# A decoder layer on one core: the first three column tiles of the gated MLP as plain products, the transformed activations made under them

## The chip, the cores and the metric

The kernel runs on one core of a Trainium2 chip. The metric is the device time of one execution in microseconds (us). The core has a matrix engine (TensorE, PE in the profile), an elementwise engine (VectorE, DVE), an engine for table functions and casts (ScalarE, ACT), a general one (GpSimd, POOL) and SyncE (SP), which here only issues transfers. Matmul results go to accumulators in PSUM, of which this kernel keeps two sets of four banks ("pa" and "pb"), each of 128 x 512 numbers.

## The reference

One decoder layer on x of 512 tokens by 2048 features. Cut to what matters:

```python
h = rmsnorm(x, g_mix) @ w_in            # four mixers on column groups: S5, Conformer, RG-LRU, pooling
x = x + concat(mixers(h)) @ w_out       # output projection and residual
h = rmsnorm(x, g_ffn)
gate, val = split(h @ w_up)             # 2048 -> 2 x 5504
gate = causal_dwconv(gate, w3, b3)      # width 3 along the tokens
x = x + (gelu(gate) * val) @ w_down     # 5504 -> 2048
out = rmsnorm(x, g_fin)
```

What follows concerns the seam between the output projection and `h @ w_up`, and the whole of `h @ w_up`.

## The kernel before

Activations are kept transposed: a row tile is 128 features by 512 tokens, sixteen of them for 2048 features. Precision is made up from a reduced 32-bit format: every operand is split into a high part (a cast, on ACT) and a low part (a subtraction, on DVE), and `mm3` (L98) issues three matmuls: high by high, high by low, low by high. Weights come in chunks of 128 x 1024 (512 KB): a load into a raw tile, the cast ("hi"), the subtraction ("lo").

**Output projection.** `quad(q, ...)` makes four of the sixteen output tiles at once in four pa banks. The last group of input rows is done in `tail` (L1037): for each q, 48 matmuls of 512 columns, then four residual additions into the tiles x2 (names A16 to A31 in the profile, pool `ar`), which free the banks, then `forms` for two pairs of row tiles and `square2`, which stores x2 to memory for the end of the layer and adds its squares to "rstd". The squares and the forms share one buffer, "hh".

**The MLP's first product.** `ffn_up` works through 43 column tiles f. Each has 128 gate and 128 value columns, and the inner dimension of 2048 is cut into two halves (even and odd row tiles; a pair p has one of each), so a tile has four weight blocks of 128 x 1024: a and b (gate, first and second half), c and d (value). Gate and value for both token halves are made in a Strassen-like way: seven products of 256 columns instead of eight. The weight forms are a, b, d as loaded, and r1 = c + d, r2 = r1 + a, r3 = c + a, r4 = r2 + b. For r1 and r3 the second block is added by an accumulating load from the GpSimd queue ("ur<-w_up"); r2 and r4 are sums on DVE. On the other side, `forms` makes for each pair p a tile X{p} of seven forms of the activations, each high and low, 256 tokens wide. A product is 24 matmuls (8 pairs by 3). The sequence per tile is a of f, d of f-1, r1 of f, r4 of f-1, r2, b, r3 of f. Sums of products are carried by accumulating in one bank and by copies on ACT: of the a bank after a (us), after a+r2 (uu) and after a+r2+r3 (uw); r1's bank is added to uw on DVE. After d and r4 the tile is finished: scaling by the norm's statistic, the convolution and the GELU, and the product with the value half, on DVE and ACT ("ug", "uc"). Each of these small tiles has two buffers. The last DVE product of a tile reads uw. The first half of the result is read straight from the a bank.

The norm's statistic need not be there before that: the weights act on x times g_ffn, and 1/rms is applied to the result. `rstd_bc` makes it: matmuls of ones with the summed squares, scaling, a square root on ACT, a reciprocal and three small steps on DVE ("tiny"), matmuls that broadcast it, a copy.

**What sets the order.** In `tail` a scheduler orders the instructions of each engine; loads and weight pieces are marked with a higher priority. Each engine then works its list in order. Raw weight tiles of `ffn_up` come from the pool `rp` with nine buffers, in the space that `ar` and `aq` leave; so the loads wait until the tiles there have been read. The d blocks use the two raw buffers of the chunk plan (`wp`); high and low parts have three buffers each (`wq`). `down`, the last product, has its weights in the chunk plan and reads the stored results back ("av", split to "Sh", "Sl"). Its first sweep accumulates in all eight banks.

## Time and profile before

| | us |
|---|---|
| median of 3 runs | 1954.33 (1952.54 to 1954.68) |
| profiled execution | 1953.47 |
| its span | 1951.7 |
| PE busy | 1869.0 (96%) |
| DVE busy | 1353.0 (69%) |
| ACT busy | 808.3 (41%) |

The span runs from the first to the last instruction; 1.8 us lie around it. The engines work beside each other, so their busy times overlap, and only what ends last in a stage sets its time. The output projection ends near 541 us, `ffn_up` runs to about 1462 us, and `down` follows it.

### The profile page before, as it was taken

Reading aid. Unit: us, or ns where it says so; the run is one execution under the profiler, and the core shown is the slowest. Engines: PE = TensorE matmul, PEld = TensorE weight load, DVE = VectorE, ACT = ScalarE, POOL = GpSimd, SP = SyncE. Lnnn points to the kernel's source line nnn. Section 1 sums busy time; section 2 is a strip of 40 time slices with the busy share of each in tenths; the row PEclk is TensorE's granted clock in tenths of the full one; section 3 lists DMA queues with packets and bytes.
Section 4 is the critical chain, followed back from the end, with each engine's and each line's share of the span. In section 5 each row is a group of like instructions: output and inputs, shape, how many; then the busy total and the mean of one; then the engine's idle time right before and its main releaser. Section 6 shows DMA issues by size and latency. Waiting matters only on the chain.

```text
span 1951.7 us, 29884 instructions
## 1 busy us (share of the span) xinstructions
PE 1869.0 (96%) x11878; PEld 1690.6 (87%) x11878; DVE 1353.0 (69%) x1997; ACT 808.3 (41%) x1064; POOL 171.3 (9%) x249
## 2 busy tenths in 40 slices
PE   7999999999928999999999999999999999999996
PEld 6788887888728999999999999999998888888886
DVE  8699989998766777777777777777765433333334
ACT  6323447432544444444444444444444222222232
POOL 6210020221001000000000000000000000000000
PEclk9999999999959999999999999999999999999998
DMA  5332323433428777776767777776738443333334
GB/s 200 99 94 89 103 90 112 142 90 94 146 78 226 190 204 188 196 204 186 209 184 206 189 195 205 190 211 182 200 100 275 135 146 108 113 108 98 98 97 141
DMA packets 106701, 298.62 MB, mean 153 GB/s; under 512 B 15233, under 2 KB 21377, under 8 KB 106561
## 3 DMA queue, kind: packets, MB, share of 16 engines
q1 hardware_dynamic: 92784, 249.78, 38.1%
q0 software_dynamic: 13488, 46.41, 14.4%
q8 instruction: 93, 1.52, 0.3%
q10 hardware_dynamic: 288, 0.52, 0.1%
q14 instruction: 48, 0.39, 0.1%
HBM read 274.51 MB, written 19.66 MB: 151 GB/s over the span
## 4 chain that ended last, share of the span: by engine, by line
PE 90%; DVE 6%; ACT 2%; DMA 1%; issue 1%; POOL 0%; DVEq 0%; POOLq 0%; ACTq 0%
PE pa L96 59%; PE pb L96 31%; DVE X L59 1%; DMA ur<-w_up 1%; DVE lo L59 1%; DVE o L59 0%; DVE rstd L59 0%; DVE bk L59 0%; DVE A L62 0%; ACT hi L105 0%; DVE l_x L62 0%; DVE M L59 0%; ACT hh L1076 0%; ACT A L72 0%; DVE A L59 0%
## 5 line engine op out<-in xcount | busy, mean ns | idle before, releaser
L96 PE MATMUL pa<-A,hi 128*128 128x512 f32 x1312 | 412.8, 397 | 11.5 <-ACT A L72 6.4
L59 DVE TENSOR_TENSOR lo<-raw,hi 128x1024 fp32r<-128x1024 f32 (+1 forms) x175 | 215.6, 1233 | 243.5 <-ACT hi L105 243.3
L105 ACT CAST hi<-raw 128x1024 fp32r<-128x1024 f32 (+1 forms) x175 | 183.0, 1046 | 458.7 <-PE pa L96 390.9
L59 DVE TENSOR_TENSOR ulr<-ur,uhr 128x1024 fp32r<-128x1024 f32 x172 | 210.4, 1223 | 149.0 <-ACT uhr L105 149.0
L96 PEld LDWEIGHTS pa<-A,hi 128*128 128x128 f32 x1312 | 247.0, 190 | 69.5 <-ACT A L72 7.3
L105 ACT CAST uhr<-ur 128x1024 fp32r<-128x1024 f32 x172 | 180.1, 1047 | 304.4 <-PE pa L96 150.4
L96 PE MATMUL pa<-X,uhr 128*128 128x256 f32 x1408 | 260.3, 285 | 6.6 <-ACT uhr L105 6.6
L96 PE MATMUL pa<-A,lo 128*128 128x512 f32 x656 | 257.5, 397 | 3.9 <-DVE lo L59 3.9
L96 PE MATMUL pb<-X,uhr 128*128 128x256 f32 x1344 | 246.4, 283 | 0.0
L96 PEld LDWEIGHTS pa<-X,uhr 128*128 128x128 f32 x1408 | 221.4, 193 | 6.8 <-ACT uhr L105 6.7
L96 PEld LDWEIGHTS pb<-X,uhr 128*128 128x128 f32 x1344 | 209.7, 192 | 0.0
L96 PE MATMUL pa<-X,ulr 128*128 128x256 f32 x704 | 200.1, 284 | 0.0
L96 PE MATMUL pb<-X,ulr 128*128 128x256 f32 x672 | 190.3, 283 | 0.0
L96 PEld LDWEIGHTS pa<-A,lo 128*128 128x128 f32 x656 | 124.4, 190 | 33.1 <-DVE lo L59 4.8
L1130 POOL DMA_DIRECT2D ur<-w_up x86 | 75.2, 874 | 857.5 <-DMA ur<-w_up 437.1
L96 PE MATMUL pa<-Sh,hi 128*128 128x512 f32 (+1 forms) x392 | 149.4, 382 | 0.0
L96 PE MATMUL pa<-Sl,hi 128*128 128x512 f32 (+1 forms) x392 | 149.2, 381 | 0.0
L96 PE MATMUL pa<-Sh,lo 128*128 128x512 f32 (+1 forms) x392 | 149.1, 381 | 0.0
L96 PEld LDWEIGHTS pa<-X,ulr 128*128 128x128 f32 x704 | 136.2, 193 | 0.0
L96 PEld LDWEIGHTS pb<-X,ulr 128*128 128x128 f32 x672 | 129.1, 192 | 0.0
L96 PE MATMUL pa<-X,uhb 128*128 128x256 f32 x688 | 126.1, 284 | 0.1
L96 PE MATMUL pb<-Sl,hi 128*128 128x512 f32 (+1 forms) x328 | 124.4, 379 | 0.0
(290 smaller groups left out, 3483.7 us busy)
## 6 DMA issues: line engine op xcount, KB each, us to landing
ur<-w_up SPq DMA_DIRECT2D x86, 512.0 KB, 5.9
ur<-w_up POOLq DMA_DIRECT2D x86, 512.0 KB, 7.3
raw<-w_dn SPq DMA_DIRECT2D x54, 512.0 KB, 3.8
ud<-w_up SPq DMA_DIRECT2D x43, 512.0 KB, 6.2
ua<-w_up SPq DMA_DIRECT2D x43, 512.0 KB, 4.7
ub<-w_up SPq DMA_DIRECT2D x43, 512.0 KB, 3.8
raw<-w_b SPq DMA_DIRECT2D x40, 512.0 KB, 3.7
raw<-w_out SPq DMA_DIRECT2D x32, 512.0 KB, 3.6
```

What stands on the lines that cost most here:

```text
L59: (eng or self.nc.vector).tensor_tensor(out, x, y, op=op)
L96: self.nc.tensor.matmul(ps, lhsT=l, rhs=r, start=start, stop=stop, skip_group_check=go_on)
L105: self.nc.scalar.copy(hi, src)
L1130: nc.gpsimd.dma_start(v8(t), blk(f, "d" if form == "r1" else "a"), accum_op=ADD)
```

## The change

Three things are changed.

1. The first three column tiles (NSTD = 3) are done in plain form by the new `ffn_std`: four weight blocks, each with all 512 tokens, eight pairs, three matmuls of 512 columns, so 96 matmuls a tile in two banks instead of 168 of 256 columns. Their weights are part of the chunk plan, behind w_out. The operand is taken from rows 0 and 6 (even row tiles) or 1 and 2 (odd row tiles) of X{p}. In the first tile, a and c take pairs 0 to 5 before 6 and 7, and `rstd_bc` stands between b and d.
2. `forms` becomes three steps. `forms1` makes the four plain forms straight from x2. `forms2` scales x2 in place and makes three of the transformed forms. `forms3` overwrites row 6, which the plain tiles read, with the last one, in the third tile. The squares get buffers of their own.
3. The residual tiles lie in pairs in the raw weight pool `rp` (now eight buffers of 128 x 1024), so a raw buffer comes free when `forms3` has read it; they are stored as eight pieces of 512 KB instead of sixteen of 256 KB. The small tiles of `ffn_up` are taken from the slots A8 to A15: us and uu become two halves of one tile (A12 and A13 in turn), uw is A14 alone, ug A8 and A9, uc A10 and A11, the statistic A15. PE's instructions of the whole tail keep the order in which the program issues them.

```diff
-MERGE = False
+NSTD = 3
...
+            self.blk = lambda f, x: a["w_up"][(NF if x in "cd" else 0) + f][:, 8 * (x in "bd"):8 * (x in "bd") + 8]
+            srcs += [self.blk(f, x) for f in range(NSTD) for x in "acbd"]
             self.plan(srcs)
...
-            self.tail()
+            with tc.manual_schedule(engines={mybir.EngineType.PE}):
+                self.tail()
...
-        self.x2 = []
+        self.x2, self.xp2 = [], []
+        self.ar.release()
+        self.rp = tc.alloc_tile_pool(name="rp", bufs=8, side="right", reuse_waits="tile")
...
-                        self.x2.append(self.at(16 + d, F32))
+                        if d % 2 == 0:
+                            self.xp2.append(self.rp.tile([P, 1024], F32, tag="raw", name=f"x2_{d}"))
+                        self.x2.append(self.xp2[-1][:, 512 * (d % 2):512 * (d % 2) + 512])
...
             for p in (2 * q, 2 * q + 1):
-                xf.append(self.forms(fx, p))
+                self.forms1(fx, p)
             for p in (2 * q, 2 * q + 1):
-                self.square2(p)
-        for pool in (ft, self.aq, self.ar):
+                self.square2(p, ft2)
+        self.ffn_std()
+        ft2.release()
+        ft.release()
+        self.ffn_up(self.xf, self.rp, self.rs)
+        for pool in (fx, self.aq, self.rp):
             pool.release()
-        with tc.tile_pool(name="rp", bufs=9, side="right", reuse_waits="tile") as rp, \
-                tc.tile_pool(name="u1", bufs=1, reuse_waits="tile") as u1, \
-                tc.tile_pool(name="up", bufs=2, reuse_waits="tile") as up:
-            self.tp = up
-            self.ffn_up(xf, rp, u1.tile([P, S], F32, name="rstd2"))
...
+    def forms1(self, pool, p):
+        t = pool.tile([P, 7, 2, 256], F32R, tag=f"X{p}", name=f"X{p}")
+        self.xf.append(t)
+        for k, sl in ((0, slice(0, 7, 6)), (1, slice(1, 3))):
+            x = self.x2[2 * p + k].rearrange("p (n c)->p n c", n=2)
+            self.split_to(t[:, sl, 0], t[:, sl, 1], x, self.prm("g_ffn", 2 * p + k))
+
+    def forms2(self, p):
+        t, r = self.xf[p], self.tmp("tr", 1024)
         for k in range(2):
+            x = self.x2[2 * p + k]
+            self.act(x, x, AF.Copy, scale=self.prm("g_ffn", 2 * p + k))
+        e, f, g, h = (self.xp2[p][:, 256 * i:256 * i + 256] for i in range(4))
+        u = r.rearrange("p (i c)->p i c", i=4)
         self.tt(u[:, 0], e, f, SUB)
+        self.tt(u[:, 2], h, f, SUB)
         self.stt(u[:, 1], u[:, 0], -1.0, h, MUL, SUB)
+        self.stt(f, u[:, 1], -1.0, g, MUL, SUB)
+        self.split_to(t[:, 3:6, 0], t[:, 3:6, 1], u[:, 0:3])
+
+    def forms3(self, p):
+        t = self.xf[p]
+        self.split_to(t[:, 6, 0], t[:, 6, 1], self.xp2[p][:, 256:512])
+
+    def ffn_std(self):
+        rows = {"a": slice(0, 7, 6), "c": slice(0, 7, 6), "b": slice(1, 3), "d": slice(1, 3)}
+        self.rs = self.at(15, F32)
+        self.actd = []
+        left = list(range(8))
+        for f in range(NSTD):
+            ps = [self.pa(), self.pb()]
+            o = [x.rearrange("p (n c)->p n c", n=2) for x in ps]
+
+            def part(x, w, p0, p1):
+                for p in range(p0, p1):
+                    c, t = slice(p * P, p * P + P), self.xf[p]
+                    self.mm3(o[x in "cd"], w[0][:, c], w[1][:, c], t[:, rows[x], 0], t[:, rows[x], 1], x in "ac" and p == 0, x in "bd" and p == 7)
+
+            if f == 0:
+                wa, wc = self.chunk(), self.chunk()
+                for p0, p1 in ((0, 6), (6, 8)):
+                    part("a", wa, p0, p1)
+                    part("c", wc, p0, p1)
+            else:
+                for x in "ac":
+                    part(x, self.chunk(), 0, 8)
+            if f == NSTD - 1:
+                for p in range(8):
+                    self.forms3(p)
+            part("b", self.chunk(), 0, 8)
+            if f == 0:
+                self.run(self.rstd_bc(self.acc, D, self.rs))
+            part("d", self.chunk(), 0, 8)
...
+            while left and len(left) > (4, 0, 0)[f]:
+                self.forms2(left.pop(0))
...
-        seq = [(0, x) for x in ("a", "r1", "b", "r2", "r3")]
-        for f in range(1, NF + 1):
+        seq = [(NSTD, x) for x in ("a", "r1", "r2", "b", "r3")]
+        for f in range(NSTD + 1, NF + 1):
...
             elif form == "r3":
-                copy(f, "a", "uw")
-                w = sv[f, "uw"]
+                sv[f, "w"] = w = self.at(14, F32)[:, 0:256]
+                nc.scalar.copy(w, bank[f, "a"][:, 0:256])
...
-        for k in range(AH + 1):
+        for k in range(AH):
...
-            if k == 0:
-                for i in range(3):
-                    product(i, 0, 6)
-            product(k, 6 if k < 3 else 0)
+            product(k)
             after(k)
-            if k == 4:
-                self.run(self.rstd_bc(self.acc, D, rstd))
```

Where this moves instructions, the lists of the engines show it. In these rows pa and pb are banks with a running number, X the forms of a pair, hi and lo (or uh and ul with the form's name) the two parts of a weight block, "x2" two instructions in a row.

PE at the seam, before: the last matmuls of the output projection (operands A12 to A15), then what follows.

```order
L96 MATMUL pa561_4975<-A14_520_4597,hi83_4893 128x512
L96 MATMUL pa561_4975<-A15_521_4598,hi83_4893 128x512
L96 MATMUL pa561_4975<-A14_520_4597,lo83_4894 128x512
L96 MATMUL pb577_5268<-ones_85,rstd_522_4631 128x1 x4
L96 MATMUL pa570_5113<-X0_4700,uha_0_5099 128x256 x2
L96 MATMUL pa570_5113<-X0_4700,ula_0_5100 128x256
L96 MATMUL pa570_5113<-X1_4715,uha_0_5099 128x256 x2
L96 MATMUL pa570_5113<-X1_4715,ula_0_5100 128x256
```

PE at the same place, after:

```order
L96 MATMUL pa533_4902<-A14_504_4593,hi83_4842 128x512
L96 MATMUL pa533_4902<-A15_505_4594,hi83_4842 128x512
L96 MATMUL pa533_4902<-A14_504_4593,lo83_4843 128x512
L96 MATMUL pa539_4992<-X0_4693,hi84_4904 128x512 x2
L96 MATMUL pa539_4992<-X0_4693,lo84_4905 128x512
L96 MATMUL pa539_4992<-X1_4698,hi84_4904 128x512 x2
L96 MATMUL pa539_4992<-X1_4698,lo84_4905 128x512
L96 MATMUL pa539_4992<-X2_4783,hi84_4904 128x512 x2
```

The ones-matmuls stood first behind the output projection, ahead of every MLP product; now the first chunk's plain products (X0, hi84) stand there.

PE between b (chunk 86) and d (chunk 87) of the first plain tile, after:

```order
L96 MATMUL pa539_4992<-X6_4967,lo86_4996 128x512
L96 MATMUL pa539_4992<-X7_4972,hi86_4995 128x512 x2
L96 MATMUL pa539_4992<-X7_4972,lo86_4996 128x512
L96 MATMUL pb541_5084<-ones_85,rstd_506_4624 128x1 x4
L96 MATMUL pb543_5096<-par_84,tiny_542_5089 128x128 x4
L96 MATMUL pb540_4993<-X0_4693,hi87_5001 128x512 x2
L96 MATMUL pb540_4993<-X0_4693,lo87_5002 128x512
```

The ones-matmuls and the broadcast (from "tiny") now follow each other with nothing between; before, the eight pairs of the first a product stood between them.

DVE in the loop, before: the rows around the last product of tile 8, which reads uw; tile 8's uc is uc_639, its product with uw the second row.

```order
L59 TENSOR_TENSOR uc_639_7068<-pb628_6709,uc_639_7068 128x256
L59 TENSOR_TENSOR uc_639_7068<-uw_635_6935,uc_639_7068 128x256
L59 TENSOR_TENSOR uld_8_7144<-ud_8_7004,uhd_8_7143 128x1024
L59 TENSOR_TENSOR ulr1_9_7178<-ur1_9_7037,uhr1_9_7177 128x1024
L59 TENSOR_TENSOR uw_643_7171<-pa638_7012,uw_643_7171 128x256
L59 TENSOR_TENSOR ulr4_8_7213<-ur4_8_7210,uhr4_8_7212 128x1024
L59 TENSOR_TENSOR ur4_9_7446<-ur2_9_7242,ub_9_7141 128x1024
L59 TENSOR_TENSOR ulr2_9_7245<-ur2_9_7242,uhr2_9_7244 128x1024
```

DVE at the same place, after: tile 8's c is A11, its product with w (A14) the sixth row.

```order
L59 TENSOR_TENSOR ur2_9_6910<-ur1_9_6706,ua_9_6641 128x1024
L59 TENSOR_TENSOR A8_601_6807<-pa600_6782,A12_597_6639 128x256
L62 SCALAR_TENSOR_TENSOR A11_599_6737<-A11_599_6737,A15_538_4991 128x512
L59 TENSOR_TENSOR uld_8_6812<-ud_8_6673,uhd_8_6811 128x1024
L59 TENSOR_TENSOR A11_599_6737<-pb589_6379,A11_599_6737 128x256
L59 TENSOR_TENSOR A11_599_6737<-A14_595_6604,A11_599_6737 128x256
L59 TENSOR_TENSOR ulr1_9_6846<-ur1_9_6706,uhr1_9_6845 128x1024
L59 TENSOR_TENSOR A14_602_6839<-pa598_6681,A14_602_6839 128x256
```

The sum for r2 of tile 9 and the low part of d of tile 8, which stood behind the product with w, now stand ahead of it (the sum for r4 stands ahead by a few more rows), and the next write of w goes to the same slot A14.

PE at the start of `down`, before: the last products of tile 42 (r4) and the first of `down` (Sh0, hi0).

```order
L96 MATMUL pa908_14969<-X7_5043,uhd_42_15129 128x256 x2
L96 MATMUL pa908_14969<-X7_5043,uld_42_15130 128x256
L96 MATMUL pb919_15299<-Sh0_15289,hi0_15276 128x512
L96 MATMUL pb920_15300<-Sh0_15289,hi0_15276 128x512
L96 MATMUL pb921_15301<-Sh0_15289,hi0_15276 128x512
L96 MATMUL pb922_15302<-Sh0_15289,hi0_15276 128x512
L96 MATMUL pa923_15303<-Sh0_15289,hi0_15276 128x512
L96 MATMUL pa925_15305<-Sh0_15289,hi0_15276 128x512
L96 MATMUL pa910_15034<-X0_4700,uhr4_42_15162 128x256 x2
```

PE at the same place, after: the sixth to eighth of the eight output tiles of the first sweep's first step.

```order
L96 MATMUL pa848_14936<-Sh0_14922,lo0_14910 128x512
L96 MATMUL pa850_14938<-Sh0_14922,hi0_14909 128x512
L96 MATMUL pa850_14938<-Sl0_14923,hi0_14909 128x512
L96 MATMUL pa850_14938<-Sh0_14922,lo0_14910 128x512
L96 MATMUL pa851_14939<-Sh0_14922,hi0_14909 128x512
L96 MATMUL pa851_14939<-Sl0_14923,hi0_14909 128x512
L96 MATMUL pa851_14939<-Sh0_14922,lo0_14910 128x512
L96 MATMUL pa849_14937<-Sh0_14922,hi0_14909 128x512
L96 MATMUL pa849_14937<-Sl0_14923,hi0_14909 128x512
L96 MATMUL pa849_14937<-Sh0_14922,lo0_14910 128x512
```

Six matmuls of `down` stood among the last Strassen products; now all Strassen products come first and the eight output tiles follow in turn, pa849 last.

## Rows read from the trace of the kernel before

**Rows 1.** The page: busy time of PE, the slices of PE and the clock

```profile
PE 1869.0 (96%) x11878; PEld 1690.6 (87%) x11878; DVE 1353.0 (69%) x1997; ACT 808.3 (41%) x1064; POOL 171.3 (9%) x249
...
PE   7999999999928999999999999999999999999996
...
PEclk9999999999959999999999999999999999999998
```

**Rows 2.** Stretches: length, busy time of each engine (instructions), clock, DMA share, GB/s

```profile
520.00:540.00 20.00, 20.00 (x89) 16.43 (x88) 17.06 (x29) 9.76 (x15) 0.00 (x0) 1.00 0.50 172
540.00:550.00 10.00, 0.74 (x4) 0.27 (x2) 6.25 (x12) 4.91 (x9) 0.00 (x0) 0.65 0.36 123
550.00:560.00 10.00, 0.00 (x0) 0.00 (x0) 6.90 (x12) 5.93 (x9) 0.00 (x0) 0.50 0.00 0
...
594.00:598.00 4.00, 4.00 (x22) 4.00 (x22) 2.87 (x3) 0.04 (x1) 0.88 (x1) 0.55 0.86 242
640.00:1400.00 760.00, 760.00 (x6336) 760.00 (x6335) 579.88 (x680) 358.19 (x454) 66.36 (x76) 1.00 0.73 197
```

**Rows 3.** Chain of waits, 470 to 640 us: start, duration, engine and work

```profile
497.77 42.99 PE pa L96 x186
...
542.60 0.61 DVE rstd L59
...
543.24 0.64 ACT hh L1076
...
576.14 4.42 DMA ur<-w_up
...
581.16 9.92 DMA ur<-w_up
...
609.53 2.88 PE pb L96 x24
```

**Rows 4.** Chain of waits, 100 to 220 us: a run of 512-column products

```profile
105.11 111.13 PE pa L96 x480
```

**Rows 5.** Timeline of PE: start, duration, instruction, [idle before, releaser]

```profile
576.98 1.84 PE L96 MATMUL pb<-ones,rstd 128*128 128x1 f32 x8 [36.24 <-DVE rstd L59]
...
584.59 1.05 PE L96 MATMUL pb<-par,tiny 128*128 128x128 f32 x8
592.20 0.80 PE L96 MATMUL pa<-X,uhr 128*128 128x256 f32 x2 [6.56 <-ACT uhr L105]
...
1454.65 0.50 PE L96 MATMUL pa<-X,uhd 128*128 128x256 f32 x2 [1.29 <-ACT uw L1162]
...
1457.62 1.10 PE L96 MATMUL pb<-Sh,hi 128*128 128x512 f32 x4
...
1461.78 0.28 PE L96 MATMUL pa<-X,ulr 128*128 128x256 f32 x1
```

**Rows 6.** Timelines of ACT and, last, DVE around the norm's statistic

```profile
500.21 0.67 ACT L72 ACTIVATE cva<-pa,half 128x512 f32<-128x512 f32 x1
...
576.02 1.03 ACT L105 CAST uha<-ua 128x1024 fp32r<-128x1024 f32 x1
577.07 1.28 ACT L72 ACT_TABLE_LOAD   x1
579.06 0.21 ACT L72 ACTIVATE tiny<-tiny 128x4 f32<-128x4 f32 x1 [0.71 <-DVE tiny L69]
...
578.94 1.23 DVE L59 TENSOR_TENSOR ula<-ua,uha 128x1024 fp32r<-128x1024 f32 x1
```

**Rows 7.** Timelines of DVE, ACT in the loop, and DVE at its end

```profile
860.12 0.42 DVE L59 TENSOR_TENSOR ug<-pa,uu 128x256 f32<-128x256 f32 x1 [0.70 <-PE pa L96]
...
866.56 0.41 DVE L59 TENSOR_TENSOR uc<-uw,uc 128x256 f32<-128x256 f32 x1
...
869.83 0.37 ACT L1162 COPY uw<-pb 128x256 f32<-128x256 f32 x1
...
1469.66 0.42 DVE L59 TENSOR_TENSOR uc<-pa,uc 128x256 f32<-128x256 f32 x1
```

More of the change, by code (lines that the diff above doesn't have):

```diff
@@ L1036, in tail @@
         ft = tc.alloc_tile_pool(name="ft", bufs=1, reuse_waits="tile")
-        self.x2d = [self.dr.tile([P, S], F32, name=f"x2d{d}") for d in range(16)]
+        ft2 = tc.alloc_tile_pool(name="ft2", bufs=2, reuse_waits="tile")
+        self.x2d = [self.dr.tile([P, 1024], F32, name=f"x2d{p}") for p in range(8)]
         self.tp = ft
         self.acc = self.tmp("rstd", pool=self.cp)
-        xf = []
+        self.xf = []
         for q in range(4):
@@ L1074, in square2 @@
             else:
-                q = self.tmp("hh", 1024)[:, 0:512]
+                q = self.tmp("sq", pool=pool)
                 self.nc.scalar.square(q, self.x2[d])
                 self.tt(self.acc, self.acc, q, ADD)
-    def forms(self, pool, p):
-        nc, t = self.nc, pool.tile([P, 7, 2, 256], F32R, tag=f"X{p}", name=f"X{p}")
-        hh, r = self.tmp("hh", 1024), self.tmp("tr", 1024)
-        v, u = hh.rearrange("p (k n c)->p k n c", k=2, n=2), r.rearrange("p (i c)->p i c", i=4)
+    def forms1(self, pool, p):
[4 more added lines that the diff above has]
+            self.split_to(t[:, sl, 0], t[:, sl, 1], x, self.prm("g_ffn", 2 * p + k))
@@ L1103, in ffn_up, with conv_gelu, keep @@
+    def conv_gelu(self, f, g, c):
+        self.act(c, g, AF.Identity, scale=self.prm("f_w", 3 * f + 2), bias=self.prm("f_b", f))
+        for d in (1, 2):
+            self.stt(c[:, d:], g[:, 0:S - d], self.prm("f_w", 3 * f + 2 - d), c[:, d:], MUL, ADD)
+        self.act(c, c, AF.Gelu_apprx_tanh)
+    def keep(self, f, c):
+        t = self.dr.tile([P, S], F32, name=f"act{f}")
+        self.nc.sync.dma_start(t, c)
+        self.actd.append(t)
     def ffn_up(self, xf, rp, rstd):
@@ L1111, in ffn_up @@
         raws, staged = {}, {}
[L1112 removed]
+        blk = self.blk
         v8 = lambda t: t.rearrange("p (k c)->p k c", k=8)
@@ L1145, in ffn_up, with product @@
         bank, sv = {}, {}
-        def product(k, p0=0, p1=8):
+        def product(k):
             f, form = seq[k]
-            wh, wl = staged[k]
+            wh, wl = staged.pop(k)
             new = form in ("a", "b", "r1")
-            if new and p0 == 0:
+            if new:
                 bank[f, form] = self.pa() if form == "b" else self.pb() if f % 2 else self.pa()
             ps = bank[f, {"a": "a", "r2": "a", "r3": "a", "d": "a", "b": "b", "r1": "r1", "r4": "r1"}[form]]
-            for p in range(p0, p1):
+            for p in range(8):
                 x, c = xf[p][:, IX[form]], slice(p * P, p * P + P)
@@ L1158, in product @@
                 self.mm(ps[:, 0:256], wl[:, c], x[:, 0], False, p == 7, True)
-        def copy(f, form, tag):
-            t = self.tmp(tag, 256)
-            nc.scalar.copy(t, bank[f, form][:, 0:256])
-            sv[f, tag] = t
         def after(k):
@@ L1167, in after @@
             if form == "a":
[L1168 removed]
+                sv[f, "s"] = self.at(12 + f % 2, F32)
+                nc.scalar.copy(sv[f, "s"][:, 0:256], bank[f, "a"][:, 0:256])
             elif form == "r2":
[L1170 removed]
+                nc.scalar.copy(sv[f, "s"][:, 256:512], bank[f, "a"][:, 0:256])
             elif form == "r3":
[L1172 to L1173 removed]
+                sv[f, "w"] = w = self.at(14, F32)[:, 0:256]
+                nc.scalar.copy(w, bank[f, "a"][:, 0:256])
                 self.tt(w, bank[f, "r1"][:, 0:256], w, ADD)
             elif form == "b":
[L1176 to L1177 removed]
+                sv[f, "g"] = self.at(8 + f % 2, F32)
+                self.tt(sv[f, "g"][:, 0:256], bank[f, "b"][:, 0:256], sv[f, "s"][:, 0:256], ADD)
             elif form == "r4":
[L1179 to L1180 removed]
+                g, c = sv[f, "g"], self.at(10 + f % 2, F32)
+                self.tt(g[:, 256:512], bank[f, "r1"][:, 0:256], sv[f, "s"][:, 256:512], ADD)
                 self.tt(g, g, rstd, MUL)
[L1182 to L1185 removed]
+                self.conv_gelu(f, g, c)
                 self.stt(c, c, -1.0, rstd, MUL, MUL)
                 self.tt(c[:, 0:256], bank[f, "a"][:, 0:256], c[:, 0:256], MUL)
[L1188 to L1193 removed]
+                self.tt(c[:, 256:512], sv[f, "w"], c[:, 256:512], MUL)
+                self.keep(f, c)
         LD, AH = 6, 2
```

39 lines of the change are left out of this document (10 added, 29 removed).

## The prediction

> **What bounds the kernel now.** I read the page's busy shares and slices first. TensorE (PE) is busy 96% of the span, and its row shows one hole: the 12th and 13th slices, with the granted clock down to 5 tenths in the first of them [rows 1]. The stretches around it give the size of the hole: from 540 to 560 us PE does next to nothing, and it idles 36.24 us up to 576.98 [rows 5], while from 640 to 1400 us it is busy the whole time with VectorE (DVE) at 76% [rows 2]. So there are two regimes: a PE-bound loop, in which only PE work counts, and one stop, in which the others count.
>
> The chain of waits names what fills the stop. Up to 540.76 it is PE (the last quad of the output projection). Then DVE adds to the sum of squares ("rstd") and ACT squares ("hh") alternate, since the squares share one buffer with the forms; after the last of them come the weight load of r1 and its accumulating partner, 4.4 and 9.9 us, since the raw buffers lie where the residual tiles were [rows 3]. PE stands 36.2 us for the last sum, and 6.56 us more for r1 [rows 5].
>
> **What the hole costs.** One Strassen product of 24 matmuls takes 2.88 us [rows 3], so 43 x 7 of them take 866.9 us. The last one ends at 1461.78 + 0.28 = 1462.06; in the loop stand one wait of 1.29 us and six matmuls of the next stage (1457.62 to 1459.02, 1.4 us) [rows 5]. The products would therefore have started without loss at 1462.06 - 866.9 - 2.7 = 592.5. Quads end at 540.8: the hole, half clock included, is worth **51.7 us**. The change can win no more than that, plus what the loop has, which is nothing.
>
> **The change, term by term.**
>
> *Hole removed: -51.7.* The plain form needs x split at once and no sums, so the first products can follow pair by pair as the pairs come. Pairs 6 and 7 come last; by the order the a and c products of pairs 0 to 5 (36 matmuls of 0.229 us, 8.2 us) stand ahead of them. The two pairs of the last quad need on DVE four residual adds and four 512-column splits of 0.6 us, with sums and one weight piece between them, so the last pair is ready some 6.8 us behind the last quad: covered, with 1.4 us to spare. The weights of these tiles come through the chunk plan right behind w_out, in buffers that no store holds, so the load waits of [rows 3] go as well. Six accumulating loads leave GpSimd's queue; the eight 512 KB stores that replace sixteen of 256 KB on SP's queue move the same bytes.
>
> *Plain work added: +5.5.* The output projection's 512-column matmuls set the price: 480 in 111.13 us, 231.5 ns each [rows 4], and 0.229 in the quads. A tile of 96 then takes 22.0 us, against 7 x 2.88 = 20.16. Three tiles: 3 x 1.84. The Trainium skill, "TensorE: Matmul & The Clock Gate", section "Back-to-back issue gap", has about 131 ns for a sustained 512-column matmul between weight loads. By that a plain tile would take 12.6 us and three would save 23 us, where the rows give a loss of 5.5; the rows decide.
>
> *Quads end later: +2.8, from 0 to 8.* PE now keeps the program's order. After 497.77 it runs nine matmuls (2.1 us) and then needs the bank whose reader, the last tanh of the GLU, ends at 500.88 [rows 6]: 1.0 us. The rest is DVE: it was busy 17 of the 20 us before the hole [rows 2], and now also makes the sums of squares and the first forms between residual adds, which release PE's banks. I take 1.8 for that; 0 if its gaps suffice, 7 if two or three forms of 1 to 3 us stand ahead of an add each quad.
>
> *The norm's statistic between b and d of tile 0: +9.3, from 4 to 12.* The ones-matmuls (half of 1.84 at full clock, 0.9), the broadcast (1.05 [rows 5]) and what lies between now stand in PE's path. On ACT, ahead of the square root, stands the cast of chunk 89, whose buffer is free only when b's product ends; then the cast of X5, the table load and the root: 1.03 + 0.8 + 1.28 + 0.21 = 3.3 us after b [rows 6]. On DVE the lo part of that chunk (1.23), one form of X5 and pieces of X6 are interleaved with the four tiny steps, about 2.3 us more. PE idles 5.7 - 0.9 = 4.8, say 4.9. Then the clock: after the 6.56 us stop the granted clock was 0.55 over 594 to 598, with 22 matmuls in 4.0 us [rows 2, 5], where 22 x 0.12 = 2.6 are due; with the start of that stretch I count 2.4 per stop. Sum 0.9 + 4.9 + 1.05 + 2.4 = 9.3. Low end: DVE lets the tiny steps through (3.4 idle) and the clock stays. High end: the interleaved pieces wait for ACT in turn. The same skill's "ScalarE: Activation LUTs", section "What ACT_TABLE_LOAD costs", adds a drain of 1.38 us to the load's 1.28; that would make this term 10.7. Here the root began 1.99 us after the load did [rows 6], under the page's 2.66.
>
> *First Strassen tile: +1, from 0 to 5.* Its raw buffers come free only when the last form is written (under tile 2, about 604), then eight loads start at once. Before, a load of r1 and its accumulation took 14.3 us [rows 3], here to about 620, against first use of r1 at 622: nearly covered by the rest of tile 2.
>
> *Loop: 0.* The copies us, uu, uw become slices of three tiles, and w has one buffer instead of two. So ACT's copy of w waits for DVE's last product with the tile before. Before, that product started 6.4 us behind the add that follows r4 (860.12) and ACT's copy 9.7 [rows 7]. In the new order three weight pieces of 1.15 us stand ahead of it, so it ends near 9.9 and the copy near 10.4; PE comes to d four products (11.5 us) behind r4's end, 11.3 behind that add. Cover 0.9 us, cost nothing; without cover every tile pays the excess, the rival below. Eight raw buffers instead of nine: the first load of a tile is then released by an add a whole product earlier than its use; hidden.
>
> *Start of down: +7.1, from 1 to 9.* Before, six matmuls of down filled PE while banks came free. Now the eighth bank's turn comes after 21 matmuls (4.9 us), and the bank is that of the last tile's a, read last of all: its reader ended 1470.08, 8.0 us behind the last product [rows 7]. With the old lag PE waits 3.1. By the new order one more split (0.6) and its load stand ahead of the reader, so I take 4.7, plus 2.4 of slow clock. Before, this wait was under other matmuls; nothing covers it now.
>
> Sum: -51.7 + 5.5 + 2.8 + 9.3 + 1 + 0 + 7.1 = **-26.0 us**. The profiled run took 1953.5 (span 1951.7 and 1.8 around it), 0.9 below the median of 1954.3, so the sum goes off either alike; from the median: **1928.3 us**.
>
> **Rivals.**
> 1. *The two new stops are nearly covered* (statistic at its low end 4, down at 1, quads +1): -51.7 + 5.5 + 1 + 4 + 1 = -40, 1914. For it: DVE's order could run ahead. Against: both waits hang on strict PE order, and neither engine ahead has slack there.
> 2. *DVE's backlog decides.* Between 500 and 565 us DVE has nearly continuous work. If it runs 5 us late, a and c of tile 0 wait about 3 us, the root 5 more, the first Strassen loads 5: -26 + 13 = -13, 1941.
> 3. *Slower: the single w buffer.* If DVE's product with w ends over 0.9 us later than I read, d waits for ACT's copy in each of 39 tiles. The gain is gone at 26/39 = 0.67 us per tile, so with the product 1.6 us later; at 1 us, +13: 1967. For it: DVE is at 76% and stands behind ACT's casts. Against: DVE has a quarter of the loop to spare [rows 2].
> 4. *The plain matmuls run faster here.* If a 512-column matmul took what a 256-column one does (0.12), a plain tile would take 11.5 and three save 26 instead of losing 5.5: 1897. All 512-column rows speak against it; it is the page's rule above as a case.
> 5. *It does not do what it says:* the stop stays because chunks or raw loads still hang on stores and PE waits some 25 us at the first Strassen tile: about 1954. Against: the first three tiles give 66 us of cover.
>
> **How the numbers follow.** Forecast 0.62 (1921 to 1937 by its terms' middle), rival 1 0.15, rival 2 0.15, slower 0.04, faster matmuls 0.01, no effect 0.03. The range takes in most of rivals 1 and 2: 1914 to 1941. A measurement of this kernel can tell about 0.2% (4 us) from no change; faster by more has 0.62 + 0.15 + 0.15 + 0.01, and the part of the single-buffer case at small excess: 0.94; within 0.2%: 0.03, no effect; slower 0.03.
>
> **What would show it.** In the changed profile: PE busy without a hole over 545 to 560; plain tiles of 22 us (0.229 each); one PE wait on DVE's tiny step near 561 to 566 of about 5 us with the clock down behind it; no long wait on the first r products near 615 to 625; products of 2.88 us through the loop, no waits on ACT's w copy; one wait of 3 to 6 us for a DVE reader at the start of down. Wrong would be: waits of d in each tile, residual adds that hold the quads for more than 8 us, or a slow clock over more than some microseconds.

## The result and the profile after

The changed kernel takes 1923.76 us (median of 4, 1921.20 to 1925.42) against 1953.63 before (median of 4 runs beside it): a ratio of 0.9846, 95% interval 0.9829 to 0.9863. That is 29.9 us faster. The forecast was 1928.3 us, 26 us faster, with a range of 1914 to 1941; the measured time lies inside it. The profiled execution took 1925.42, its span is 1923.6, 28.1 us less than the span before; the account below is made against that.

The page: PE's hole in the 12th and 13th slices [rows 1] is gone, and the granted clock shows no dip at this grain.

```profile
PE   8999999999999999999999999999999999999996
...
PEclk9999999999999999999999999999999999999998
```

The stretches, with the columns of [rows 2]: length, busy time of PE, PEld, DVE, ACT and POOL (instructions), clock, DMA share, GB/s.

```profile
520.00:540.00 20.00, 19.53 (x86) 15.58 (x85) 20.00 (x34) 17.41 (x27) 0.00 (x0) 1.00 0.57 198
540.00:550.00 10.00, 10.00 (x46) 8.29 (x45) 10.00 (x17) 8.58 (x13) 0.00 (x0) 1.00 0.46 168
550.00:560.00 10.00, 10.00 (x46) 8.28 (x45) 9.97 (x18) 6.19 (x9) 0.00 (x0) 1.00 0.38 120
560.00:570.00 10.00, 5.83 (x29) 5.14 (x28) 7.83 (x20) 5.19 (x7) 0.00 (x0) 0.79 0.33 107
640.00:1400.00 760.00, 760.00 (x6335) 760.00 (x6335) 560.59 (x677) 365.48 (x452) 65.49 (x75) 1.00 0.73 195
```

From 540 to 560 PE is now busy throughout, where it had 0.74 of 20 us before [rows 2], and DVE is busy for nearly all of that time beside it. One stop is left, between 560 and 570. The loop shows no idle PE either way.

All PE waits from 500 us, in the output projection, to the start of down (what was waited for: us in total, times, longest):

```profile
PE pb L96 <- DVE tiny L62: 4.2, 1, 4.2
PE pa L96 <- DVE A L59: 2.9, 1, 2.9
PE pb L96 <- ACT uhr L105: 2.0, 1, 2.0
PE pa L96 <- ACT cva L72: 1.6, 1, 1.6
PE pa L96 <- ACT A L1234: 1.3, 1, 1.3
PE pb L96 <- DVE ulr L59: 0.8, 1, 0.8
PE pa L96 <- DVE x L59: 0.5, 1, 0.5
```

Where [rows 5] had stops of 36.24 and 6.56 us, the longest is now 4.2. The places, in PE's timeline (start, duration, instruction, idle before and its releaser): the first plain tile from its start, with the norm's statistic and d, to the start of the second; then the first Strassen products; then the first matmul of down and the one that needs the late bank.

```profile
545.36 0.61 PE L96 MATMUL pa<-X,hi 128*128 128x512 f32 x2
...
566.80 2.08 PE L96 MATMUL pb<-par,tiny 128*128 128x128 f32 x8 [4.17 <-DVE tiny L62]
568.53 1.20 PE L96 MATMUL pb<-X,hi 128*128 128x512 f32 x2
...
576.00 0.62 PE L96 MATMUL pa<-X,hi 128*128 128x512 f32 x2
```

```profile
619.52 0.40 PE L96 MATMUL pb<-X,uha 128*128 128x256 f32 x2
...
624.55 0.50 PE L96 MATMUL pb<-X,uhr 128*128 128x256 f32 x2 [1.99 <-ACT uhr L105]
625.81 0.38 PE L96 MATMUL pb<-X,ulr 128*128 128x256 f32 x1 [0.76 <-DVE ulr L59]
```

```profile
1430.72 0.40 PE L96 MATMUL pb<-Sh,hi 128*128 128x512 f32 x1
...
1438.72 0.50 PE L96 MATMUL pa<-Sh,hi 128*128 128x512 f32 x1 [2.93 <-DVE A L59]
```

### The profile page after: what moved, and what is told of

Its sections match the earlier page's. It is cut to its first block, busy times and chain, and to the rows that moved or that the text cites. A ratio compares the mean times of both kernels' runs of the same rounds, so it can differ in the third digit from the quotient of the medians.

```text
span 1923.6 us, 29377 instructions
## 1 busy us (share of the span) xinstructions
PE 1875.6 (98%) x11662; PEld 1683.5 (88%) x11662; DVE 1313.1 (68%) x1978; ACT 808.5 (42%) x1054; POOL 164.5 (9%) x243
## 4 chain that ended last, share of the span: by engine, by line
PE 89%; DVE 6%; DMA 2%; ACT 2%; issue 1%; POOL 0%; DVEq 0%; SPq 0%; ACTq 0%; POOLq 0%
PE pa L96 57%; PE pb L96 31%; DVE lo L59 1%; DMA ur<-w_up 1%; ACT hi L105 1%; DVE X L59 1%; DMA av<-act 1%; DVE M L59 0%; DVE bk L59 0%; DMA raw<-w_dnt 0%; ACT L72 0%; DVE l_x L62 0%; DVE A L59 0%; DVE pr L59 0%; DVE A L62 0%
## 5 line engine op out<-in xcount | busy, mean ns | idle before, releaser
L59 DVE TENSOR_TENSOR lo<-raw,hi 128x1024 fp32r<-128x1024 f32 (+1 forms) x187 | 231.0, 1236 | 275.9 <-ACT hi L105 275.7
L105 ACT CAST hi<-raw 128x1024 fp32r<-128x1024 f32 (+1 forms) x187 | 195.6, 1047 | 503.9 <-PE pa L96 423.9
L105 ACT CAST uhr<-ur 128x1024 fp32r<-128x1024 f32 x160 | 167.6, 1047 | 262.0 <-PE pb L96 129.0
L59 DVE TENSOR_TENSOR ulr<-ur,uhr 128x1024 fp32r<-128x1024 f32 x160 | 195.5, 1222 | 116.9 <-ACT uhr L105 116.9
L96 PE MATMUL pb<-X,uhr 128*128 128x256 f32 x1280 | 233.9, 283 | 2.0 <-ACT uhr L105 2.0
L96 PE MATMUL pa<-X,uhr 128*128 128x256 f32 x1280 | 233.8, 283 | 0.0
L96 PEld LDWEIGHTS pa<-X,uhr 128*128 128x128 f32 x1280 | 199.7, 192 | 0.0
L96 PE MATMUL pa<-X,ulr 128*128 128x256 f32 x640 | 181.1, 283 | 0.0
L96 PE MATMUL pb<-Sh,hi 128*128 128x512 f32 (+1 forms) x328 | 125.3, 382 | 0.0
L96 PE MATMUL pb<-Sh,lo 128*128 128x512 f32 (+1 forms) x328 | 125.1, 381 | 0.0
```

Source lines behind the costliest of these rows:

```text
L59: (eng or self.nc.vector).tensor_tensor(out, x, y, op=op)
L96: self.nc.tensor.matmul(ps, lhsT=l, rhs=r, start=start, stop=stop, skip_group_check=go_on)
L105: self.nc.scalar.copy(hi, src)
```

## The sum again, with measured terms

This is an account of two spans, so it must close; what it tests is the size of each term.

The first plain product starts at 545.36, so the quads end 4.6 us later than the 540.76 of before. Of this, 1.5 us is older than the change: an instruction that stands in the same place in both lists, the first of the GLU's matmuls, starts at 483.10 before and 484.64 after, behind the same rows of PE in both. In the other kernels of this case it starts at 482.0 to 486.4, so this is scatter. So 3.1 belong to the seam. (The GLU is the gated unit of the S5 mixer; "cva" is its tanh.) The first plain tile runs from 545.36 to 576.00, 30.64 us; the third ends at 619.52, so tiles two and three take 43.52, 21.76 each. The Strassen products run from 619.52 to 1430.72: 811.2, of which 280 products of 2.88 are 806.4, the waits at the first r product 1.99 + 0.76, and one wait in the last tile 1.29, as long as before [rows 5]. What lies behind the last product takes 492.9 us against 491.0 before (1951.7 less 1462.06, plus the 1.4 us of down's matmuls that stood earlier).

| term | forecast | measured |
|---|---|---|
| hole removed | -51.7 | -51.7 (read from before) |
| scatter ahead of the seam | - | +1.5 |
| quads end later | +2.8 | +3.1 |
| three plain tiles | +5.5 | +4.8 (3 x 1.60) |
| the norm's statistic | +9.3 | +8.9 (30.64 - 21.76) |
| first Strassen tile | +1 | +2.75 of waits, 0.8 beside them |
| loop | 0 | 0 |
| start of down and after | +7.1 | +1.8 |
| sum | -26.0 | -28.1 |

## The experiments

Times are medians; ratios are to the kernel before, run beside each.

**1. One cause of the stop alone: squares in a buffer of their own, in the kernel before.**

```diff
+        ft2 = tc.alloc_tile_pool(name="ft2", bufs=1, reuse_waits="tile")
...
-                q = self.tmp("hh", 1024)[:, 0:512]
+                q = self.tmp("sq", pool=pool)
```

> The kernel before with one edit: the squares of the residual tiles get a 512-column buffer of their own instead of sharing hh with the forms. Theory (the stop is two things in a row: squares and forms in turns on one buffer, then the loads that wait for the last residual tile): only the first part shrinks. DVE had about 10 us of idle pieces of 0.7 us in the stop, so the last sum comes 8 to 10 us earlier and the loads with it: 1944 to 1946, and PE still idles about 25 us plus the wait for r1. Rival (the forms themselves set the stop's length, buffers do not matter): within 2 us of before. Second rival (only the loads matter): within 2 us as well, but with the loads issued at the same time.

Measured: 1935.4, ratio 0.9906 (0.9891 to 0.9921), -18 us: the theory's direction, twice its size. PE's timeline in that run (columns as above):

```profile
555.71 1.83 PE L96 MATMUL pb<-ones,rstd 128*128 128x1 f32 x8 [14.12 <-DVE rstd L59]
563.52 2.05 PE L96 MATMUL pb<-par,tiny 128*128 128x128 f32 x8 [5.97 <-DVE tiny L62]
...
575.06 0.79 PE L96 MATMUL pa<-X,uhr 128*128 128x256 f32 x2 [5.48 <-ACT uhr L105]
```

The wait for the last sum fell from 36.24 [rows 5] to 14.12, more than the 0.7 us gaps that I had counted. In DVE's timeline of before the sums of squares stand in groups of four (542.5 to 547.4, 557.3 to 562.1, 572.0 to 576.8) with the forms of two pairs between them: the shared buffer set not only the turns inside a group but kept the groups apart. The r1 product moved from 592.20 [rows 5] to 575.06. What is left is serial too: the sum, the tiny steps (5.97) and the load (5.48), 25.6 us of waits. The edit also turned PE's list: here the broadcast stands ahead of the first a products, so the tiny steps show as a wait, which they were not before [rows 5]. The buffer alone brought three fifths of what the change gains.

**2. The converse: the squares share a buffer again, in the changed kernel.**

```diff
-                q = self.tmp("sq", pool=pool)
+                q = self.tmp("tr", 1024)[:, 0:512]
```

> The changed kernel with one edit: the squares share the buffer tr with the forms again. Sharing cost the kernel before about 18 us (run sq_own). Theory (under the plain tiles the squares and the later forms have some 60 us of cover, so what held PE before holds it no more; by the order the later forms now all stand behind the last square): within 3 us of the changed kernel, 1921 to 1927. Rival (the buffer of their own is what brought most of the gain, the plain tiles little): 1935 or more, with PE waiting for the last sum near 561 us.

Measured: 1922.6, 0.9845 (0.9829 to 0.9862), no difference to the change. So the changed kernel does not need the buffer, and the two gains do not add. It is not shown that the plain tiles alone would hide the turns of before, for here these do not come back: the last square is at 551.37 on ACT, and the first cast of a later form stands behind it, at 553.89. What the plain tiles cover is seen in the changed kernel: its last sum of squares ends at 555.67, 10.3 us behind the quads and no earlier than in experiment 1 (555.56). There PE had waited 14.12 us for it; here PE works on plain products until it needs the sum at 561.68, and does not wait.

**3. Two plain tiles instead of three.**

```diff
-NSTD = 3
+NSTD = 2
...
-            while left and len(left) > (4, 0, 0)[f]:
+            while left and len(left) > (0, 0, 0)[f]:
```

> The changed kernel with two plain tiles instead of three (all later forms made in the first). Theory (a plain tile costs 21.76 us against 20.16, and the third one covers nothing that the second could not: forms3 keeps its place half a tile ahead of the first Strassen product): 1.6 us less, 1921 to 1923, the wait for r1 as before, about 2.8 us. Rival (the third tile is needed as cover for the forms or the first loads): 3 us or more slower, 1927 up, with a longer wait at the first r1 product.

Measured: 1922.6, 0.9846 (0.9826 to 0.9866). The forecast difference of 1.6 us is too small for these runs, which spread over 8 us; the rival (over 3 us slower) is not seen. The wait at the first r product was 1.66 + 0.76 us, against 1.99 + 0.76 with three tiles. Whether the third tile costs its 1.6 us stays open; that it is not needed as cover is shown.

**4. The broadcast behind d.**

```diff
             if f == 0:
-                self.run(self.rstd_bc(self.acc, D, self.rs))
+                norm = self.rstd_bc(self.acc, D, self.rs)
+                assert next(norm) == "PE"
+                while next(norm) != "PE":
+                    pass
             part("d", self.chunk(), 0, 8)
+            if f == 0:
+                self.run(norm)
```

> The changed kernel with one edit: the ones-matmuls of the norm's statistic stay between b and d of the first tile, the broadcast goes behind d. Theory (the stop of 4.2 us there is DVE and ACT work that d's 24 matmuls can cover, 5.4 us): the wait goes to under 1 us and the half clock behind it with it, about -6 us against the changed kernel: 1917 to 1919. Rival (PE then waits as long behind d, or for the second tile's banks, since the first tile's results are scaled later): within 2 us of the changed kernel.

Measured: 1916.1, 0.9805 (0.9792 to 0.9818), 7.6 us below the change. PE's timeline at the place:

```profile
558.98 0.95 PE L96 MATMUL pb<-ones,rstd 128*128 128x1 f32 x8
...
565.36 1.05 PE L96 MATMUL pb<-par,tiny 128*128 128x128 f32 x8
```

The broadcast has no idle time ahead of it, and its 8 records take 1.05 us, where they took 2.08 in the changed kernel behind the stop. So the stop's whole price is shown: 4.17 us of idle and, at half clock, 0.9 under the broadcast and 2.0 under d, 7.1 in all for 7.6 gained.

**5. The late bank of down taken up later.**

```diff
...
+                    def out(k, ds):
...
+                    if g == sw == 0 and f == 0:
+                        cw = {0: self.chunk(), 1: self.staged[1]}
+                        out(0, range(7))
+                        out(1, range(5))
+                        out(0, [7])
+                    else:
+                        cw = {f: self.chunk()}
+                        out(f, range(5, 8) if g == sw == 0 and f == 1 else range(8))
```

Here `out(k, ds)` issues the output tiles ds of step k.

> The changed kernel with one edit: at the start of down the output tile whose bank comes free last is taken up after five output tiles of the second step. Theory (the wait of 2.9 us and the half clock behind it are the price of that bank alone): PE reaches it 3.5 us later, no wait over 0.5 us there, about -4.5 us against the changed kernel: 1918 to 1920. Rival (the split of the second step's activations or its weights is late too, so the wait moves ahead by a few matmuls): within 2 us of the changed kernel, with a wait for Sl or lo.

Measured: 1917.2, 0.9817 (0.9804 to 0.9830), 6.6 us below the change by the medians, 5.7 by the ratios. What is left of PE's wait there (as above):

```profile
PE pa L96 <- DVE A L59: 0.9, 1, 0.9
```

2.93 us became 0.9, the granted clock stayed at 1.00 behind it, and the second step's operands were in time. The wait (2.0) and the half clock (1.6, see below) make 3.6 us; in the two profiled executions what lies behind the last Strassen product is 4.3 us shorter (488.6 against 492.9). The rest of the 6.6 is within the scatter, for the four runs of each kernel spread over some 4 us.

**6. Both.** The two edits above together.

> The changed kernel with both edits, the broadcast behind d and the late bank taken up later. Theory (two separate stops): the gains add up, about -11 us against the changed kernel, 1912 to 1914. Rival (the first edit only moves time to the second place or to the start of the first Strassen tile, where raw loads then come too late by as much): less than 7 us gained.

Measured: 1911.6, 0.9786 (0.9772 to 0.9799): 12.1 us below the change, where the single edits gave 7.6 and 6.6. They add up within the scatter of these runs; the spans of the profiled executions fell by 13.7, and by 8.2 and 4.7 for the single edits.

**7. The strict order of PE taken back in the whole tail.**

```diff
-            with tc.manual_schedule(engines={mybir.EngineType.PE}):
-                self.tail()
+            self.tail()
```

> The changed kernel with one edit: the scheduler orders PE in the tail again. In its list the broadcast of the norm's statistic stands behind the whole a product of the second tile, and six matmuls of down stand among the last Strassen products. Theory (the strict order costs two stops, 4.2 us and 2.9 us of waiting, each with about 2.2 us of half clock, and gains 3.2 us at the end of the kernel): -11.5 + 3.2, so 8 us faster than the changed kernel, about 1916; no wait over 2 us at the broadcast and at the start of down, a wait of 4 to 5 us on the last sum of squares. Rival (without the strict order another stop appears, since b or c of the first tile is then pulled ahead of pairs that are not ready): 1924 or more, with a wait of PE for X near 545 to 556 us.

Measured: 1910.4, 0.9780 (0.9765 to 0.9794), 13.4 us below the change; expected were 8. Its PE waits over the seam, the loop and the start of down:

```profile
PE pb L96 <- ACT uhr L105: 1.4, 1, 1.4
PE pa L96 <- ACT A L1233: 1.3, 1, 1.3
PE pa L96 <- ACT A L72: 0.8, 1, 0.8
PE pb L96 <- DVE ulr L59: 0.8, 1, 0.8
```

The wait on the last sum of squares is 4.57 us, as forecast. No wait at the broadcast, none at the start of down, and none on the tanh ("cva") of the GLU, which I had not set down to the strict order's account in this run's expectation although the forecast names it. From the first matmul of the GLU to the first plain product PE takes 56.1 us here (485.95 to 542.05) and 60.7 in the changed kernel. These 4.6 us, waits and half clock, are most of the 5.4 that were not expected. So the one part of the change that the profile speaks against is the strict order of PE, the last stage apart (experiment 8); the plain tiles and the pools need no such order.

**8. The end of the kernel alone: strict order there, in the kernel before.**

```diff
-        self.down2()
+        with self.tc.manual_schedule(engines={mybir.EngineType.PE}):
+            self.down2()
```

> The kernel before with one edit: PE keeps the program's order in the last stage (the last 16 of the down product's inner steps and the final norm). Theory (the change gained about 3.2 us there, since the broadcast of the first half's norm comes earlier and DVE's scaling no longer delays the last residual add): the wait of PE on the last sum of squares falls from 4.6 to about 1.4 us, 1950 to 1951. Rival (that difference between the two traces has another cause, such as the timing of the loads): 1953 to 1954, wait still over 4 us.

Measured: 1950.8 (10 runs), 0.9984 (0.9974 to 0.9993), -2.5 us. PE's timeline at the final norm, before and in this run:

```profile
1924.89 0.50 PE L96 MATMUL pb<-ones,rstd 128*128 128x1 f32 x4
...
1929.40 0.61 PE L96 MATMUL pb<-par,tiny 128*128 128x128 f32 x4
...
1936.72 1.01 PE L96 MATMUL pb<-ones,rstd 128*128 128x1 f32 x4 [4.56 <-DVE rstd L59]
```

```profile
1922.51 0.61 PE L96 MATMUL pb<-ones,rstd 128*128 128x1 f32 x4 [0.81 <-DVE rstd L59]
...
1925.93 0.69 PE L96 MATMUL pb<-par,tiny 128*128 128x128 f32 x4
```

The broadcast of the first half's norm comes 3.4 us behind its ones-matmuls instead of 4.5 and stands further ahead of the last product in PE's list. In the chain of waits of before, DVE's scaling of that half (1930.04, 5.38 us) ended right ahead of the last residual add (1935.42); now it starts earlier, and the last ones-matmuls (at 1933.80) wait 1.42 us instead of 4.56; in the changed kernel they wait 1.42 too. That is the gain at the end which the forecast did not have.

**9 and 10. How much room the single w buffer has.** Two DVE operations more in each Strassen tile ahead of the product that reads w: on data that is no longer read (slack_in), or in the product's own chain (slack_out).

```diff
+                for _ in range(2):
+                    self.tt(g[:, 0:256], g[:, 0:256], g[:, 256:512], ADD)
                 self.tt(c[:, 256:512], sv[f, "w"], c[:, 256:512], MUL)
```

> The changed kernel with two more DVE operations of 256 columns in each Strassen tile, on data that is no longer read; by the order both stand ahead of the product that reads w, without moving any other piece ahead of it: 0.68 us later. Theory (1.1 us to spare in front of that bank, and 26 per cent of DVE): no change, within 2 us of the changed kernel, no PE wait in the loop. Rival (there is less to spare than the trace shows, the added DVE work costs as such): each 0.1 us over the slack would cost 4 us, and if all of it counts 27 us.

```diff
+                for _ in range(2):
+                    self.tt(c[:, 256:512], c[:, 256:512], c[:, 256:512], mybir.AluOpType.max)
                 self.tt(c[:, 256:512], sv[f, "w"], c[:, 256:512], MUL)
```

> The changed kernel with two more DVE operations of 256 columns (0.34 us each) in the chain ahead of the product that reads w, in each of the 40 Strassen tiles; by the order one low part of a weight (1.14 us) then also stands ahead of it, so that product ends about 1.8 us later. The maximum of a value with itself leaves the result as it is. Theory (one buffer for w leaves 1.1 us until PE needs the bank, 0.9 by the prediction): the excess of 0.7 us is paid in each of 39 tiles, +28 us, about 1950 (1944 to 1958), with a PE wait on ACT's copy in every tile. Rival (the loop has other slack: PE is not held, or the order of the pieces shifts once and then no more): within 3 us of the changed kernel.

Measured: slack_in 1994.2, 1.0208 (1.0194 to 1.0221); slack_out 1990.4, 1.0187 (1.0172 to 1.0202). The smaller delay cost as much as the larger one, 70 and 67 us over the change: my account of room (1.1 us, then 0.1 us for each 0.1 over it) fell, and with it both forecasts. PE's waits in slack_in:

```profile
PE pa L96 <- ACT A L1234: 31.0, 20, 1.6
PE pb L96 <- ACT A L1234: 28.2, 18, 1.6
```

A wait of 1.6 us in each of 38 tiles, for ACT's copy of w (L1234). The timelines of ACT show why, first in the changed kernel, then in slack_in, both from the cast for r1 of a tile on:

```profile
859.02 1.05 ACT L105 CAST uhr<-ur 128x1024 fp32r<-128x1024 f32 x1 [1.83 <-PE pa L96]
860.34 0.37 ACT L1234 COPY A<-pa 128x256 f32<-128x256 f32 x1 [0.27 <-DVE A L59]
862.24 1.05 ACT L105 CAST uhr<-ur 128x1024 fp32r<-128x1024 f32 x1 [1.52 <-PE pb L96]
863.19 0.36 ACT L1229 COPY A<-pb 128x256 f32<-128x256 f32 x1
```

```profile
856.98 1.05 ACT L105 CAST uhr<-ur 128x1024 fp32r<-128x1024 f32 x1 [1.83 <-PE pb L96]
859.86 1.04 ACT L105 CAST uhr<-ur 128x1024 fp32r<-128x1024 f32 x1 [1.83 <-PE pa L96]
860.81 0.37 ACT L1229 COPY A<-pa 128x256 f32<-128x256 f32 x1
861.08 0.38 ACT L1234 COPY A<-pb 128x256 f32<-128x256 f32 x1
```

And DVE's product that frees w, in each:

```profile
859.84 0.42 DVE L59 TENSOR_TENSOR A<-A,A 128x256 f32<-128x256 f32 x1
```

```profile
858.47 0.41 DVE L59 TENSOR_TENSOR A<-A,A 128x256 f32<-128x256 f32 x1
```

In the changed kernel the copy of w (860.34) follows right behind DVE's product (859.84 + 0.42). In slack_in the product ends at 858.88, 0.66 us later in its tile as planned, but the copy comes at 861.08, 2.2 us after that. It stands behind the cast for r4, which waits for a product of PE, and the copy of the next a bank (L1229). The scheduler, which builds ACT's list ahead of the run, had put it there. In slack_out the copy has the same place in the list (857.11, behind the cast for r4 at 855.90 and the copy of the next a bank at 856.85) and PE the same wait of 1.56 us. So what the delay changed was an order, and the price is that order's, not the delay's: a tile of slack_in takes 21.97 us instead of 20.16, 1.81 more, of which 1.56 is the wait and the rest I have not placed.

**11. The same load without the single buffer.** w in the two halves of its tile in turn, in slack_in:

```diff
+        wt = self.at(14, F32)
...
-                sv[f, "w"] = w = self.at(14, F32)[:, 0:256]
+                sv[f, "w"] = w = wt[:, 256 * (f % 2):256 * (f % 2) + 256]
```

> The run slack_in (two more DVE operations of 256 columns per Strassen tile) with one edit: w is kept in the two halves of A14 in turn, so ACT's copy of w waits for PE alone. In slack_in the scheduler had put ACT's copy of w behind the cast for r4 and the copy of the next a bank, and PE waited 1.56 us in each tile for it. Theory (the cost of slack_in is the order that the single buffer made, not the added DVE work): the copy stands ahead of the cast for r4 again, no wait of PE in the loop, within 3 us of the changed kernel, 1921 to 1927. Rival (the DVE work itself, 0.68 us per tile, holds PE at another place): 1950 or more.

Measured: 1924.5, 0.9856 (0.9841 to 0.9870), the change's time with the added DVE work in it. ACT's copy of w (857.64) stands ahead of the cast for r4 (859.56) again, and the loop has no PE wait. That settles it: 0.68 us more of DVE per tile cost nothing, the order that the single buffer brought cost 70 us.

**12. The best version found.** Experiments 7 and 8 together: the scheduler orders PE in the tail, strict order in the last stage alone.

> The changed kernel with PE ordered by the scheduler in the tail except for its last stage, where PE keeps the program's order. Theory (the strict order costs at the seam and at the start of down and gains at the end, three separate places): no_manual's 1910.4 less the 2.5 to 3.2 us of end_manual, 1907 to 1908. Rival (the end's gain needs the strict order in the stages ahead too): 1909 to 1912.

Measured: 1909.0, 0.9775 (0.9761 to 0.9790), 44 us below the kernel before and 15 below the change. Its trace has the end's wait at 1.4 us in place of 4.6, and in the two profiled executions what lies behind the last Strassen product is 3.1 us shorter (486.6 against 489.7). The time is within the scatter of experiment 7's 1910.4, so by the times the addition of the two is likely and not shown.

## Why the prediction was right, step by step

**The hole.** Right: PE is busy where it stood. Experiment 1 confirms the cause as named (squares and forms on one buffer, then the loads): 18 us went with the buffer, and three waits of 25.6 us stayed, the last of them for a load. In the changed kernel PE has plain products over what is left of them. Which share of the 18 us the plain tiles would hide alone, without the new order of the forms, no run shows.

**Plain tiles.** 226.7 ns per matmul instead of 229, so 4.8 instead of 5.5. The Trainium skill ("TensorE: Matmul & The Clock Gate", section "Back-to-back issue gap") has about 131 ns for such a stream. The rows of both kernels speak against it, and so against rival 4.

**Quads.** 3.1 for 2.8, but the split was wrong, and that the sum came out is luck. I took 1.0 for the GLU's banks and 1.8 for DVE. The trace has 3.1 us of waits on the GLU's results (0.81 and 0.23 at 496, 0.48 at 498.7 and 1.63 at 501.3) and one wait of 0.5 on a residual add (the last in the list of waits above): DVE was full, 20.00 of 20 us, and still in time. A wait on the GLU's inputs is 0.4 shorter than before (1.55 for 1.97). Half clock, which this term left out, adds nothing to the difference: the clock was 0.50 from 502 to 504 after, and from 492 to 494 before.

**The norm's statistic.** 8.9 for 9.3: 0.95 for the ones, 4.17 idle, 1.73 for the broadcast and 2.03 of half clock under d. The idle time was 0.7 shorter than forecast and the half clock, 0.9 of the broadcast's 1.73 counted in, 0.5 dearer. The timeline of ACT in the changed kernel has the chain as it was read from the order:

```profile
561.65 1.04 ACT L105 CAST hi<-raw 128x1024 fp32r<-128x1024 f32 x1 [3.65 <-PE pa L96]
562.60 0.83 ACT L105 CAST X<-tr 128x768 fp32r<-128x768 f32 x1
563.45 1.28 ACT L72 ACT_TABLE_LOAD   x1
564.74 0.20 ACT L72 ACTIVATE tiny<-tiny 128x4 f32<-128x4 f32 x1
```

The cast waits until b ends, then come the cast of X5, the table load and the root. The Trainium skill ("ScalarE: Activation LUTs", section "What ACT_TABLE_LOAD costs") adds a drain of 1.38 us to the load. The root starts 1.29 us after the load's start here, so this trace has none.

**First Strassen tile.** +1 was too low: 2.75 us of waits. The step that failed is the load: forms3 freed the buffers as read, but the loads start at 606.4, where I had 604, and the two loads of r1 took 6.14 + 10.24 = 16.4 us in the chain, where I had the 14.3 of [rows 3]. They landed at 623.4 instead of 620, and the cast, DVE's sum (623.38, 1.23 us) and its split stood behind them:

```profile
606.38 6.14 DMA ur<-w_up
...
613.12 10.24 DMA ur<-w_up
```

**Loop.** Zero, as forecast, but for a reason half understood. The cover was there (ACT's copy of w ended at 860.71, and the bank was due 11.3 us behind r4's add at 850.50, at 861.8) and yet no measure of safety: rival 3 priced the loss as the excess over it, in each of 39 tiles (39 us at 1 us, so 13 slower than before), and experiments 9 to 11 show a step of 70 / 39 = 1.8 us per tile as soon as the list turns over.

**Down.** +7.1 was the term most in error; measured is +1.8. Three things: the wait was 2.93 instead of 4.7 (the lag of the late bank stayed at 8.0 us, the old lag, from which the forecast had 3.1 before it added for the new order); the half clock cost 1.6 instead of 2.4 (nine matmuls from 1439.52 to 1443.16, 3.64 us where 2.07 are due); and the strict order won 2.5 us at the end of the kernel (experiment 8), a place that the forecast took as untouched although the change orders PE there too. These give 2.93 + 1.6 - 2.5 = 2.0.

**The sum.** The mechanism of each main term is as forecast, but that the sum is within some 2 us of the spans' difference is in part luck: down came out 5.3 lower, and the first Strassen tile 2.6 higher and the scatter of 1.5 go against it.

**Rivals.** Rival 1 (both stops covered) did not come by itself, but experiments 4 to 6 made it: 1911.6, where it had 1914. Rivals 2, 4 and 5 are not seen, and rival 3 not in the change itself.

## What to carry to other kernels

A stop of one engine is worth its length only once: work put over it and the removal of its causes do not add. Here a buffer of its own for the squares brought three fifths of the gain without any work over the stop, and nothing once the work and the new order of the forms were there. An order that is fixed by hand costs at every place where the next instruction is not ready; in the last stage of this kernel it paid, so fix it only for stages where it was measured to pay. And room in front of a buffer is safe only as far as the engines' lists stay as they are: after any edit compare the lists, not only the margins in us.

## What the runs showed of the hardware that was not expected

The half clock behind a stop is not a fixed price. After 4.17 us of idle PE the granted clock was 0.50 over the broadcast and the first half of d, the lower of the two levels (1.2 instead of 2.4 GHz), and cost 2.9 us. At the start of down, with 2.93 us of idle, the clock came down only while PE was working again, and cost 1.6 us:

```profile
1436.00:1438.00 2.00, 0.00 (x0) 0.00 (x0) 2.00 (x4) 1.15 (x2) 0.00 (x0) 1.00 0.72 248
1438.00:1440.00 2.00, 1.28 (x5) 1.04 (x6) 0.96 (x3) 0.00 (x0) 0.00 (x0) 0.91 0.77 256
1440.00:1442.00 2.00, 2.00 (x7) 1.51 (x6) 0.82 (x2) 1.73 (x3) 0.00 (x0) 0.50 0.40 144
```

It was 1.00 through the stop and fell within the second of these stretches, some 1 us after PE had begun again.

Nor does the length of the stop alone decide whether the clock falls. The waits of 1.99 and 0.76 us at the first r product left it at 1.00 in every stretch of 2 us from 620 to 630. In experiment 4 the same place has shorter waits, 1.60 and 0.76 us, and the clock fell behind them:

```profile
616.00:618.00 2.00, 2.00 (x11) 2.00 (x11) 2.00 (x4) 1.12 (x2) 0.00 (x0) 0.50 1.02 309
```

A wait of 1.63 us in the output projection (501.3, behind shorter ones from 496 on) was followed by 0.50 too, while the waits of 1.6 us in slack_in, one in each tile, left the stretch from 640 to 1400 at 1.00. The forecast charged 2.4 us per stop; its two stops cost 2.9 and 1.6.
